# Two decoder layers on one core: weight matrices laid out block by block in DRAM

## The chip, the cores and the metric

The kernel runs on one core of a Trainium2 chip. The metric is the time of one execution on the device in microseconds (us), as a median of several runs. One further execution was profiled. Its trace gives the span from the first to the last instruction, what each engine did and waited for, and what the 16 DMA engines moved.

## The reference, cut to what matters

Two decoder layers, width 2048, sequence 256, all in float32. In each layer the input is scaled and shifted by vectors that come from a conditioning vector `c`, goes through a token mixer with 16 heads, and is added back through a gate and normalized. An MLP with hidden width 8192 does the same.

```python
c_act = jax.nn.silu(c)
for l in range(DEPTH):                                   # DEPTH = 2
    mod = c_act @ w_ada[l] + b_ada[l]                    # w_ada[l]: 2048 x 12288
    sh_a, sc_a, g_a, sh_m, sc_m, g_m = jnp.split(mod[:, None, :], 6, axis=-1)
    h = x * (1.0 + sc_a) + sh_a
    y = _mixer(h, ..., w_in[l], ..., w_o[l], ...)        # w_in[l]: 2048 x 6152, w_o[l]: 2048 x 2048
    x = _layernorm(ALPHA * x + (1.0 + g_a) * y, ln1_g[l], ln1_b[l])
    h = x * (1.0 + sc_m) + sh_m
    y = jnp.square(jax.nn.relu(h @ w_up[l])) @ w_down[l] # 2048 x 8192, 8192 x 2048
    x = _layernorm(ALPHA * x + (1.0 + g_m) * y, ln2_g[l], ln2_b[l])
```

The mixer splits `h @ w_in` into queries, keys and values of two groups of 8 heads and, between them, 8 columns of forget gates (`ff`), runs causal attention in both groups, and multiplies the joined heads by `w_o`.

## The kernel before

All weights are read once, in loads of 512 KB, each into a buffer `raw` of 128 partitions x 1024 float32 (4 KB on each partition). There are 7 such buffers (`RAW_BUFS`), used in turn, and every load is issued by SP, so all of them stand in one queue in the order of the program. SP issues a load once the buffer that it goes to has been read for the last time.

There are three kinds of load:

- **Blocks of a weight matrix** (`w_in`, `w_o`, `w_up`, `w_down`): 256 rows by 512 columns. `rows_of` (L348) cuts them out of the row-major matrix, and `wload` (L138) issues them at L140. Row p of the block and row 128+p go to partition p, so a partition gets two runs of 2 KB. There are 768 of them. For each, ACT rounds the block into `wh` (L134), DVE takes the rest into `wl` (L135), and PE runs three matmuls for each product (`mm3` at L302 to L304, `proj_T` at L328 to L331, `up` at L908 and L910), so that the result has nearly full float32 precision. `wh` and `wl` have three buffers each.
- **Scale and shift loads**, `ada_T` (L150, issued at L156): 128 rows of `w_ada`, from each of which two runs of 512 columns are taken, one of the shift and one of the scale, 2048 columns apart. Again two runs of 2 KB for each partition. 256 of them. DVE multiplies each by one element of `c_act` for each partition and adds it up (L146, L148); after 16 loads PE and DVE reduce the sum over the partitions.
- **Gate loads**, `ada_G` (L179, issued at L189): 128 rows of `w_ada`, 1024 neighbouring columns, so one run of 4 KB for each partition. 128 of them, added up by the same line L148.

The blocks set the order of the program. `block` (L289) is called for each of them, and before it issues its load, it lets other work take a step: attention tasks, pieces put off (`later`), and `side_step`, which issues the `w_ada` loads at a rate that is set for each stage (`RATES`). One small load stands apart: `forget` (L697) reads the 8 forget-gate columns of `w_in` at L700, as runs of 32 bytes, 16 of them for each partition.

At the start, 16 scale and shift loads must have been added up before the first `h` can be made. The first three of them are issued, then two loads of `x`, then the bias of `w_ada` (tile `r`, L120), which PE transposes and DVE copies (L124), and only then the other 13.

Of the kernel before, what the change touches and what calls it, by code (L numbers as in the profile page):

```python
# [18 lines left out]
P = 128  # L19
D = 2048  # L20
S = 256
NT = S // P
KT = D // P
DEPTH = 2
HD = 128
NF = 8
# [3 lines left out]
GRP = 2048  # L30
# [7 lines left out]
CW = 512  # L38
OFF_FQ, OFF_FK, OFF_FV = 0, FW, 2 * FW
OFF_FF = 3 * FW  # L40
OFF_DQ = OFF_FF + NF
OFF_DK = OFF_DQ + FW
OFF_DV = OFF_DK + FW
RAW_BUFS = 7
# [26 lines left out]
    return math.ldexp(float(round(m * 2**bits)), e - bits)  # L71

@with_exitstack
def decoder(ctx: ExitStack, tc: tile.TileContext, x, c, positions, w_ada, b_ada, w_in, b_f,
            lambda_q1, lambda_k1, lambda_q2, lambda_k2, subln_g, w_o, ln1_g, ln1_b, w_up, w_down,
            ln2_g, ln2_b, out):
    nc = tc.nc
# [72 lines left out]
    def ada_T(l, vec, kt0):  # L150

        acc = gp.tile([P, 2, CW], F32, tag="acc", name="acc", bufs=1)
        for kt in range(KT):
            raw = wp.tile([P, 2, CW], F32, tag="raw", name="rawa", bufs=RAW_BUFS)
            rows = w_ada[l, kt * P:(kt + 1) * P, :].rearrange("p (v n) -> p v n", n=D)
            nc.sync.dma_start(raw, rows[:, vec:vec + 2, kt0 * P:kt0 * P + CW])  # L156
            ada_add(acc, raw, kt, kt == 0)
            if kt < KT - 1:
                yield 1

        def finish():
            pss = []
            for i in range(2):
                ps = bank()
                for f in range(4):
                    nc.tensor.transpose(ps[:, f * P:(f + 1) * P], acc[:, i, f * P:(f + 1) * P], ident)
                pss.append(ps)
            yield
            for i, ps in enumerate(pss):
                red = sm.tile([P, 4], F32, tag="red", name="red")  # L170
                nc.vector.reduce_sum(red, ps.rearrange("p (f k) -> p f k", f=4), axis=mybir.AxisListType.X)
                s0 = (vec + i) * KT + kt0
                nc.vector.scalar_tensor_tensor(modT[l, vec + i][:, kt0:kt0 + 4], red, float(i),
                                               badaT[l][:, s0:s0 + 4], ALU.add, ALU.add)

        pending[(l, vec, kt0)] = [0, finish()]
        yield 1

    def ada_G(l, vec):  # L179

        gates[l, vec] = []
        for half in range(2):
            c0 = vec * D + half * 1024
            acc = gp.tile([P, 1024], F32, tag="acc", name="acc", bufs=1)
            nc.gpsimd.memset(acc, 0.0)
            nc.sync.dma_start(acc[0:1, :], b_ada[l:l + 1, c0:c0 + 1024])
            for kt in range(KT):
                raw = wp.tile([P, 1024], F32, tag="raw", name="rawa", bufs=RAW_BUFS)
                nc.sync.dma_start(raw, w_ada[l, kt * P:(kt + 1) * P, c0:c0 + 1024])  # L189
                ada_add(acc, raw, kt, False)  # L190
                if kt < KT - 1:
                    yield 1
            hi, lo = split_w(acc.unsqueeze(1), 1, 1024)
            g = g4([P, 1024], f"gate{l}_{vec}_{half}")
            gates[l, vec].append(g)

            def finish(g=g, hi=hi, lo=lo):
                for q in range(2):
                    qs = slice(q * CW, (q + 1) * CW)
                    ps = bank()  # L200
                    nc.tensor.matmul(ps, lhsT=ones_r, rhs=hi[:, 0, qs], start=True, stop=False)
                    nc.tensor.matmul(ps, lhsT=ones_r, rhs=lo[:, 0, qs], start=False, stop=True)
                    nc.scalar.activation(g[:, qs], ps, AF.Identity, bias=one)
                yield

            pending[(l, vec, "gate", half)] = [0, finish()]
            yield 1
# [98 lines left out]
    def proj(po, lhs, wrows, c0, kt0, kt1, first=True, last=True):  # L306

        for kb in range(kt0, kt1, 2):
            wh, wl = block(wrows(kb, 2, c0, CW), 2, CW)
            need_h(kb + AHEAD)  # L310
            for j in range(2):
                kt = kb + j
                for t in range(NT):
                    mm3(po[t], lhs(kt, 0, t), lhs(kt, 1, t), wh[:, j, :], wl[:, j, :],
                        first and kt == kt0, last and kt == kt1 - 1)

    def proj_T(po, hT, wrows, c0, kt0, kt1, first=True, last=True):


        for kb in range(kt0, kt1, 2):  # L320
            wh, wl = block(wrows(kb, 2, c0, CW), 2, CW)
            need_h(kb + AHEAD)
            for j in range(2):
                kt = kb + j
                for f in range(4):
                    cs = slice(f * P, (f + 1) * P)
                    o = po[f // 2][:, (f % 2) * S:(f % 2 + 1) * S]
                    nc.tensor.matmul(o, lhsT=wh[:, j, cs], rhs=hT[:, kt, 0, :],  # L328
                                     start=first and kt == kt0 and f % 2 == 0, stop=False)
                    nc.tensor.matmul(o, lhsT=wh[:, j, cs], rhs=hT[:, kt, 1, :], start=False, stop=False)  # L330
                    nc.tensor.matmul(o, lhsT=wl[:, j, cs], rhs=hT[:, kt, 0, :], start=False,  # L331
                                     stop=last and kt == kt1 - 1 and f % 2 == 1)

    def proj_tail(po, lhs, wrows, c0, kt0, kt1, done):


        room = big.tile([P, 4, 2, 2, CW], F32R, tag="hT", name="room")
        ws = []
        for i, kb in enumerate(range(kt0, kt1, 2)):
            ws.append(block(wrows(kb, 2, c0, CW), 2, CW, (room[:, i, 0], room[:, i, 1]) if i < 4 else None))  # L340
        for t in range(NT):
            for kt in range(kt0, kt1):
                wh, wl = ws[(kt - kt0) // 2]
# [1 line left out]
                mm3(po[t], lhs(kt, 0, t), lhs(kt, 1, t), wh[:, j, :], wl[:, j, :], False, kt == kt1 - 1)  # L345
            done(t)

    def rows_of(w):  # L348
        def f(kb, a, c0, n):
            return w[kb * P:(kb + a) * P, c0:c0 + n].rearrange("(a p) n -> p a n", p=P)  # L350
        return f


    mask = const.tile([P, 2, P], F32, name="mask")
# [342 lines left out]
    def forget(l, hT):  # L697

        raw = wp.tile([P, KT, NF], F32, tag="raw", name="fraw", bufs=RAW_BUFS)
        nc.sync.dma_start(raw, w_in[l, :, OFF_FF:OFF_FF + NF].rearrange("(a p) n -> p a n", p=P))  # L700
        wf = wp.tile([P, KT, 2 * NF], F32R, tag="wh", name="wf", bufs=W_BUFS)
        nc.scalar.copy(wf[:, :, 0:NF], raw)
        nc.vector.tensor_sub(wf[:, :, NF:2 * NF], raw, wf[:, :, 0:NF].bitcast(F32))
# [51 lines left out]

    def mixer(l, hT, gate_key, stats, passes, done):

        wr = rows_of(w_in[l])

        def lhs(kt, part, t):  # L760
            return hT[:, kt, part, t * P:(t + 1) * P]
# [109 lines left out]
            return (MXf if kt < 8 else MXd)[:, kt % 8, part, t * P:(t + 1) * P]  # L871

        side_rate(RATES[l][2])
        wo = rows_of(w_o[l])

        def finish(ch, po, t):
            add_gated(po, gate_key, ch, stats, True, [t])
# [16 lines left out]

    def mlp(l, hT, gate_key, stats, done, halves, pieces):

        wu = rows_of(w_up[l])

        def up(c0, kt0, kt1):
            pu = [mm(), mm(), bank(), bank()]  # L900
            for kb in range(kt0, kt1, 2):
                wh, wl = block(wu(kb, 2, c0, CW), 2, CW)
                need_h(kb + AHEAD)
                for j in range(2):
                    kt = kb + j
# [33 lines left out]
        for g in range(NG):  # L939
# [24 lines left out]
            def lhs(kt, part, t):  # L964
                return Hs[kt // 8][:, kt % 8, part, t * P:(t + 1) * P]

            wd = rows_of(w_down[l, g * GRP:(g + 1) * GRP, :])
            last = g == NG - 1
            for ch in range(4):
                po = [mm() for _ in range(NT)]  # L970
# [79 lines left out]
    for l in range(DEPTH):  # L1050
# [30 lines left out]
        mlp(l, hT, (l, 5), old, after, halves if early_up else None, affine_later(ln1_g[l:l + 1], ln1_b[l:l + 1]))  # L1081


_INS = ["x", "c", "positions", "w_ada", "b_ada", "w_in", "b_f", "lambda_q1", "lambda_k1", "lambda_q2",
        "lambda_k2", "subln_g", "w_o", "ln1_g", "ln1_b", "w_up", "w_down", "ln2_g", "ln2_b"]


# [16 lines left out]
```

## Time and profile before

| | |
|---|---|
| Median of 3 runs | 2371.37 us (2369.19 to 2372.78) |
| The profiled execution | 2369.32 us, of which the span is 2367.6 us |
| PE busy | 2281.3 us, 96% of the span |
| DVE, ACT busy | 1790.1 us (76%), 1155.3 us (49%) |
| DMA | 619.37 MB, mean 262 GB/s; packets took 77.6% of the time of 16 engines |
| Mean granted TensorE clock | 0.994 |

How to read it: PE is TensorE's matmuls, DVE VectorE, ACT ScalarE, SPq the queue of SyncE that issues the DMAs. `a <- b: t, n, m` in a table of waits means that a waited for b, t us in total, n times, m us at the longest. In the chain of waits, each piece is what the next one had to wait for; a DMA in it has its start of issue and the time until it landed. A DMA share is the part of the time in which the mean of the 16 DMA engines had a packet in work; it can read slightly over 1. A clock of 1.00 is the full 2.4 GHz, 0.50 is 1.2 GHz.

### The profile page before, as it was taken

The numbers are of one execution on the slowest core, as the hardware profiler recorded it, in microseconds if no ns is written. First come the engines' busy times: TensorE is split into PE (matmuls) and PEld (weight loads), VectorE is DVE, ScalarE is ACT, GpSimd is POOL, SyncE is SP. The second block draws the span as 40 slices with busy tenths as digits, with TensorE's granted clock in tenths as the row PEclk, the third lists the DMA queues.
The fourth block names the chain that finished last, engine by engine and source line by source line (L and its number), as shares of the span: only waits on it lengthen the run. The fifth ranks groups of instructions, "written<-read, shape, count | busy, mean of one in ns | idle before, by whom it ended". The sixth has DMA issues, their size and how long they took to land.

```text
span 2367.6 us, 33293 instructions
## 1 busy us (share of the span) xinstructions
PE 2281.3 (96%) x12444; PEld 1959.6 (83%) x12444; DVE 1790.1 (76%) x2339; ACT 1155.3 (49%) x1684; POOL 35.1 (1%) x60
## 2 busy tenths in 40 slices
PE   4999999899999999999999999999999999999998
PEld 3878798699989888888777778987888888888886
DVE  7899888988888778888777975667675666555657
ACT  2543675344546345346444663444554553553542
POOL 0000010000000000000000000000000000000000
PEclk9999999999999999999999999999999999999999
DMA  9999688889898888888759877765777777756653
GB/s 344 326 331 308 193 265 305 312 315 325 303 349 301 302 281 309 312 293 300 273 186 303 292 226 234 233 215 170 221 263 251 229 242 240 230 189 195 187 188 123
DMA packets 309890, 619.37 MB, mean 262 GB/s; under 512 B 24200, under 2 KB 25048, under 8 KB 309728
## 3 DMA queue, kind: packets, MB, share of 16 engines
q1 hardware_dynamic: 309728, 617.25, 77.6%
q8 instruction: 97, 1.59, 0.3%
q14 instruction: 65, 0.53, 0.1%
HBM read 615.07 MB, written 2.10 MB: 261 GB/s over the span
## 4 chain that ended last, share of the span: by engine, by line
PE 76%; DVE 9%; DMA 9%; issue 3%; ACT 2%; POOL 0%; SPq 0%; DVEq 0%; ACTq 0%; POOLq 0%
PE mm L303 13%; PE mm L302 13%; PE mm L304 13%; PE mm L908 7%; PE bank L908 7%; DMA rawa<-in_w_ada_dram 5%; PE mm L331 4%; PE mm L330 4%; PE mm L328 4%; PE mm L910 4%; PE bank L910 4%; DVE wl L135 4%; DVE acc L148 2%; DMA raw<-in_w_in_dram 1%; ACT wh L134 1%
## 5 line engine op out<-in xcount | busy, mean ns | idle before, releaser
L134 ACT CAST wh<-raw 128x1024 fp32r<-128x1024 f32 x752 | 789.5, 1052 | 929.5 <-PE mm L304 491.5
L135 DVE TENSOR_TENSOR wl<-raw,wh 128x1024 fp32r<-128x1024 f32 x752 | 913.7, 1221 | 347.2 <-ACT wh L134 343.9
L148 DVE SCALAR_TENSOR_TENSOR acc<-rawa,cact,acc 128x1024 f32<-128x1024 f32 x368 | 471.0, 1280 | 137.8 <-DMA rawa<-in_w_ada_dram 136.5
L303 PE MATMUL mm<-wl,Hs 128*128 128x512 f32 x992 | 386.5, 390 | 2.0 <-DVE wl L135 1.9
L302 PE MATMUL mm<-wh,Hs 128*128 128x512 f32 x992 | 386.2, 389 | 0.0
L304 PE MATMUL mm<-wh,Hs 128*128 128x512 f32 x992 | 386.0, 389 | 0.0
L331 PE MATMUL mm<-hT,wl 128*128 128x256 f32 x1024 | 289.6, 285 | 6.0 <-DVE wl L135 5.4
L328 PE MATMUL mm<-hT,wh 128*128 128x256 f32 x1024 | 290.9, 285 | 1.9 <-DVE hT L486 1.1
L330 PE MATMUL mm<-hT,wh 128*128 128x256 f32 x1024 | 289.8, 284 | 0.2 <-DVE hT L487 0.2
L908 PE MATMUL mm<-hT,wh 128*128 128x512 f32 x768 | 286.7, 396 | 0.5 <-DVE hT L487 0.5
L908 PE MATMUL bank<-hT,wh 128*128 128x512 f32 x768 | 286.2, 395 | 0.0
L303 PEld LDWEIGHTS mm<-wl,Hs 128*128 128x128 f32 x992 | 186.2, 188 | 41.9 <-DVE wl L135 3.5
L302 PEld LDWEIGHTS mm<-wh,Hs 128*128 128x128 f32 x992 | 186.2, 188 | 38.7
L304 PEld LDWEIGHTS mm<-wh,Hs 128*128 128x128 f32 x992 | 186.2, 188 | 38.6
L910 PE MATMUL mm<-hT,wl 128*128 128x256 f32 x768 | 215.5, 281 | 0.2 <-DVE wl L135 0.2
L910 PE MATMUL bank<-hT,wl 128*128 128x256 f32 x768 | 215.3, 280 | 0.0
L302 PE MATMUL mm<-wh,hT 128*128 128x512 f32 x512 | 200.8, 400 | 5.9 <-DVE hT L486 5.7
L303 PE MATMUL mm<-wl,hT 128*128 128x512 f32 x512 | 203.4, 397 | 3.1 <-DVE wl L135 2.7
L331 PEld LDWEIGHTS mm<-hT,wl 128*128 128x128 f32 x1024 | 196.0, 192 | 8.7 <-DVE wl L135 8.3
L304 PE MATMUL mm<-wh,hT 128*128 128x512 f32 x512 | 200.9, 393 | 0.0
L328 PEld LDWEIGHTS mm<-hT,wh 128*128 128x128 f32 x1024 | 196.8, 192 | 3.4 <-DVE hT L486 1.3
L330 PEld LDWEIGHTS mm<-hT,wh 128*128 128x128 f32 x1024 | 197.1, 192 | 0.8 <-DVE hT L487 0.4
(248 smaller groups left out, 2665.7 us busy)
## 6 DMA issues: line engine op xcount, KB each, us to landing
rawa<-in_w_ada_dram SPq DMA_DIRECT2D x384, 512.0 KB, 5.5
raw<-in_w_up_dram SPq DMA_DIRECT2D x256, 512.0 KB, 4.8
raw<-in_w_down_dram SPq DMA_DIRECT2D x256, 512.0 KB, 5.1
raw<-in_w_in_dram SPq DMA_DIRECT2D x192, 512.0 KB, 5.4
raw<-in_w_o_dram SPq DMA_DIRECT2D x64, 512.0 KB, 4.6
gb<-in_ln_g_dram SPq DMA_DIRECT2D x12, 256.0 KB, 5.5
bb<-in_ln_b_dram SPq DMA_DIRECT2D x12, 256.0 KB, 5.3
xacc<-in_x_dram SPq DMA_DIRECT2D x8, 256.0 KB, 6.7
```

The costliest lines, as they stand in the source:

```text
L134: nc.scalar.copy(wh, raw)
L135: nc.vector.tensor_sub(wl, raw, wh.bitcast(F32))
L148: nc.vector.scalar_tensor_tensor(acc, raw, k, acc, ALU.mult, ALU.add)
L302: nc.tensor.matmul(o, lhsT=hi, rhs=wh, start=start, stop=False)
L303: nc.tensor.matmul(o, lhsT=hi, rhs=wl, start=False, stop=False)
L304: nc.tensor.matmul(o, lhsT=lo, rhs=wh, start=False, stop=stop)
L328: nc.tensor.matmul(o, lhsT=wh[:, j, cs], rhs=hT[:, kt, 0, :], start=first and kt == kt0 and f % 2 == 0, stop=False)
L330: nc.tensor.matmul(o, lhsT=wh[:, j, cs], rhs=hT[:, kt, 1, :], start=False, stop=False)
L331: nc.tensor.matmul(o, lhsT=wl[:, j, cs], rhs=hT[:, kt, 0, :], start=False, stop=last and kt == kt1 - 1 and f % 2 == 1)
L908: nc.tensor.matmul(pu[f], lhsT=wh[:, j, cs], rhs=hT[:, kt].rearrange("p a s -> p (a s)"), start=kt == kt0, stop=False)
L910: nc.tensor.matmul(pu[f][:, 0:S], lhsT=wl[:, j, cs], rhs=hT[:, kt, 0, :], start=False, stop=kt == kt1 - 1)
```

## The change

The host stores the weights in another order, and the kernel reads them in that order. `w_in` (without its 8 forget-gate columns), `w_o`, `w_up` and `w_down` become arrays of blocks: block [column group of 512][pair of 128-row groups] holds [128 partitions][2][512], as it will stand in `raw`. A block is then 512 KB in one piece, and each partition's part is a run of 4 KB. `w_ada` is split into two arrays, one for the scale and shift loads (`w_ada_T`, [partition][2][512] for each load) and one for the gate loads (`w_ada_G`, [partition][1024] for each load), both in one piece of 512 KB for each load. The forget-gate columns become an array `w_f` with 512 bytes in one run for each partition. The loads, their sizes, their tiles, their order and all computation stay as they were.

```diff
-OFF_DQ = OFF_FF + NF
+OFF_DQ = OFF_FF
...
-            rows = w_ada[l, kt * P:(kt + 1) * P, :].rearrange("p (v n) -> p v n", n=D)
-            nc.sync.dma_start(raw, rows[:, vec:vec + 2, kt0 * P:kt0 * P + CW])
+            nc.sync.dma_start(raw, w_ada_T[l, vec // 3, kt0 // 4, kt])
...
-                nc.sync.dma_start(raw, w_ada[l, kt * P:(kt + 1) * P, c0:c0 + 1024])
+                nc.sync.dma_start(raw, w_ada_G[l, vec // 3, half, kt])
...
-            wh, wl = block(wrows(kb, 2, c0, CW), 2, CW)
+            wh, wl = block(wrows(kb, c0), 2, CW)
...
-    def rows_of(w):
-        def f(kb, a, c0, n):
-            return w[kb * P:(kb + a) * P, c0:c0 + n].rearrange("(a p) n -> p a n", p=P)
-        return f
+    def blocks_of(w, first=0):
+
+        return lambda kb, c0: w[c0 // CW, (first + kb) // 2]
...
-        nc.sync.dma_start(raw, w_in[l, :, OFF_FF:OFF_FF + NF].rearrange("(a p) n -> p a n", p=P))
+        nc.sync.dma_start(raw, w_f[l])
...
-            wd = rows_of(w_down[l, g * GRP:(g + 1) * GRP, :])
+            wd = blocks_of(w_down[l], g * GRP // P)
...
+def _blocks(w):
+
+    l, k, n = w.shape
+    return w.reshape(l, k // 256, 2, P, n // CW, CW).transpose(0, 4, 1, 3, 2, 5)
+
+
+def _laid_out(inputs):
+
+    t = dict(inputs)
+    a = t.pop("w_ada")
+    a = a.reshape(DEPTH, KT, P, 2, 3, D)
+    t["w_ada_T"] = a[:, :, :, :, 0:2].reshape(DEPTH, KT, P, 2, 2, 4, CW).transpose(0, 3, 5, 1, 2, 4, 6)
+    t["w_ada_G"] = a[:, :, :, :, 2].reshape(DEPTH, KT, P, 2, 2, D // 2).transpose(0, 3, 4, 1, 2, 5)
+    w = t["w_in"]
+    t["w_f"] = w[:, :, OFF_FF:OFF_FF + NF].reshape(DEPTH, KT, P, NF).transpose(0, 2, 1, 3)
+    t["w_in"] = _blocks(np.concatenate([w[:, :, :OFF_FF], w[:, :, OFF_FF + NF:]], axis=2))
+    for name in ("w_o", "w_up", "w_down"):
+        t[name] = _blocks(t[name])
+    return t
```

The new order is made on the host before the launch, outside the time measured.

## Rows read from the trace of the kernel before

**Rows 1.** The page: span, and DMA packets of the whole execution.

```profile
span 2367.6 us, 33293 instructions
...
DMA packets 309890, 619.37 MB, mean 262 GB/s; under 512 B 24200, under 2 KB 25048, under 8 KB 309728
```

**Rows 2.** Waits of PE over the whole span, two rows.

```profile
PE mm L303 <- DVE wl L135: 6.4, 8, 1.7
...
PE mm L331 <- DVE wl L135: 5.4, 5, 2.0
```

**Rows 3.** Waits of PE in six stretches, one row each, in order of time.

```profile
PE mm L303 <- DVE wl L135: 1.7, 1, 1.7
...
PE mm L303 <- DVE wl L135: 1.5, 1, 1.5
...
PE mm L303 <- DVE wl L135: 1.2, 2, 0.9
...
PE mm L303 <- DVE wl L135: 1.5, 3, 0.8
...
PE mm L331 <- DVE wl L135: 3.6, 3, 2.0
...
PE mm L331 <- DVE wl L135: 1.4, 1, 1.4
```

**Rows 4.** The chain of waits in order of time: start us, us, what.

```profile
3.93 7.23 DMA r<-in_b_ada_dram
...
250.85 5.22 DMA raw<-in_w_in_dram
...
444.09 1.21 DVE xacc L497 x2
...
1131.54 5.96 DMA rawa<-in_w_ada_dram
...
1248.83 5.64 DMA rawa<-in_w_ada_dram
...
1307.49 6.59 DMA raw<-in_w_in_dram
...
1440.54 5.65 DMA raw<-in_w_in_dram
...
1525.44 5.48 DMA rawa<-in_w_ada_dram
```

**Rows 5.** Lines L156 and L189: issue ns min/median/max, and time to landing.

```profile
L156 SPq DMA_DIRECT2D rawa<-in_w_ada_dram x256: 367/368/554, 1.3 to 1555.3; - x128
...
DMA to landing us min/median/max: 3.5/5.6/10.4
...
L189 SPq DMA_DIRECT2D rawa<-in_w_ada_dram x128: 327/341/933, 200.1 to 2009.1; - x128
...
DMA to landing us min/median/max: 3.4/5.4/7.6
```

**Rows 6.** Busy time by stretch; last three columns: granted clock, DMA share, GB/s.

```profile
0.00:237.00 237.00, 200.38 (x1024) 167.56 (x1025) 202.61 (x243) 96.88 (x121) 5.04 (x29) 1.00 0.95 327
...
500.00:560.00 60.00, 59.86 (x501) 59.62 (x500) 49.15 (x47) 25.39 (x31) 0.00 (x0) 1.00 0.97 343
...
660.00:690.00 30.00, 30.00 (x134) 24.84 (x133) 25.36 (x26) 13.36 (x16) 0.00 (x0) 1.00 1.01 374
...
1340.00:1400.00 60.00, 59.10 (x304) 46.98 (x302) 49.20 (x126) 39.02 (x102) 4.65 (x4) 1.00 0.73 223
```

**Rows 7.** The same view, three short stretches (first time: PE busy).

```profile
1448.00:1452.00 4.00, 4.00 (x23) 4.00 (x22) 1.68 (x2) 0.23 (x1) 0.00 (x0) 0.57 0.95 309
260.00:268.00 8.00, 7.07 (x26) 4.88 (x25) 7.99 (x28) 4.15 (x12) 0.00 (x0) 0.79 0.44 136
...
1242.00:1244.00 2.00, 2.00 (x10) 1.67 (x9) 2.00 (x3) 0.78 (x1) 0.00 (x0) 1.00 0.73 84
```

**Rows 8.** DMA queue in 2160 to 2240 us, then in 2265 to 2325 us.

```profile
q1 hardware_dynamic: 7817, 15.09, 64.1%
...
q1 hardware_dynamic: 5925, 11.41, 56.3%
```

More of the change, by code (lines that the diff above doesn't have):

```diff
@@ L73, in decoder @@
 @with_exitstack
-def decoder(ctx: ExitStack, tc: tile.TileContext, x, c, positions, w_ada, b_ada, w_in, b_f,
+def decoder(ctx: ExitStack, tc: tile.TileContext, x, c, positions, w_ada_T, w_ada_G, b_ada, w_in, w_f, b_f,
             lambda_q1, lambda_k1, lambda_q2, lambda_k2, subln_g, w_o, ln1_g, ln1_b, w_up, w_down,
@@ L320, in proj_T @@
         for kb in range(kt0, kt1, 2):
-            wh, wl = block(wrows(kb, 2, c0, CW), 2, CW)
+            wh, wl = block(wrows(kb, c0), 2, CW)
             need_h(kb + AHEAD)
@@ L339, in proj_tail @@
         for i, kb in enumerate(range(kt0, kt1, 2)):
-            ws.append(block(wrows(kb, 2, c0, CW), 2, CW, (room[:, i, 0], room[:, i, 1]) if i < 4 else None))
+            ws.append(block(wrows(kb, c0), 2, CW, (room[:, i, 0], room[:, i, 1]) if i < 4 else None))
         for t in range(NT):
@@ L756, in mixer @@
     def mixer(l, hT, gate_key, stats, passes, done):
-        wr = rows_of(w_in[l])
+        wr = blocks_of(w_in[l])
         def lhs(kt, part, t):
@@ L873, in mixer @@
         side_rate(RATES[l][2])
-        wo = rows_of(w_o[l])
+        wo = blocks_of(w_o[l])
         def finish(ch, po, t):
@@ L895, in mlp @@
     def mlp(l, hT, gate_key, stats, done, halves, pieces):
-        wu = rows_of(w_up[l])
+        wu = blocks_of(w_up[l])
         def up(c0, kt0, kt1):
@@ L901, in up @@
             for kb in range(kt0, kt1, 2):
-                wh, wl = block(wu(kb, 2, c0, CW), 2, CW)
+                wh, wl = block(wu(kb, c0), 2, CW)
                 need_h(kb + AHEAD)
@@ L1081, in decoder @@
         mlp(l, hT, (l, 5), old, after, halves if early_up else None, affine_later(ln1_g[l:l + 1], ln1_b[l:l + 1]))
-_INS = ["x", "c", "positions", "w_ada", "b_ada", "w_in", "b_f", "lambda_q1", "lambda_k1", "lambda_q2",
-        "lambda_k2", "subln_g", "w_o", "ln1_g", "ln1_b", "w_up", "w_down", "ln2_g", "ln2_b"]
+_INS = ["x", "c", "positions", "w_ada_T", "w_ada_G", "b_ada", "w_in", "w_f", "b_f", "lambda_q1", "lambda_k1",
+        "lambda_q2", "lambda_k2", "subln_g", "w_o", "ln1_g", "ln1_b", "w_up", "w_down", "ln2_g", "ln2_b"]
+def _blocks(w):
[13 more added lines that the diff above has]
+    return t
 def kernel(**inputs):
@@ L1093 @@
     arrays, args = {}, []
+    inputs = _laid_out(inputs)
     for name in _INS:
```

## The prediction

> **What bounds the kernel now.** I read the page first: the table of the time before has PE busy for 96% of the span, and 619 MB moved by DMA engines that are busy for 77.6% of it [rows 1]. Both are near their ends, so the question is which of them still makes the other wait. The chain of waits puts some 9% of the span on DMAs, but a chain shows one tight path, and another may stand right behind it. So I went from the chain to PE's own waits. A faster load can shorten the run only where PE stands still, or where its clock falls, because a load is late.
>
> PE's waits for weights are waits for `wl`, the last thing made from a block: 6.4 and 5.4 us, 13 times in all [rows 2]. Six stretches hold 10.9 of these 11.8 us [rows 3]: 440 to 450 us (1.7), 1100 to 1150 (1.5), 1224 to 1275 (1.2), 1300 to 1320 (1.5), 1405 to 1450 (3.6) and 1500 to 1560 (1.4). The reader is to see how small that is: a queue that moves 619 MB costs PE about 12 us in 2368. In the stretch 0 to 237 us the DMA engines are busy for 95% of the time, and still no such wait is among the six [rows 6].
>
> For each stretch I then asked the chain of waits, in order of time, what stands ahead of the late `wl` [rows 4]. Five times it is a run of loads, each issued when the one before it had been used up: 4 loads up to the one at 1131.54, 5 up to 1248.83, one of `w_in` at 1307.49 (behind broadcasts of layer-norm rows that the change doesn't touch), 5 up to 1440.54, 4 up to 1525.44. In the first stretch it is not a load: DVE is adding into `xacc` (444.09), one instruction behind the other. Those 1.7 us are not the change's to win.
>
> **The change part by part.** *Packets.* Before, 309890 − 25048 = 284842 packets have 2 KB or more [rows 1]. If each run is one packet, the 1024 loads with runs of 2 KB make 262144, the 128 gate loads with runs of 4 KB 16384; that leaves 6314, which fits the 40 loads of `x` and layer-norm rows and the 8 stores of the output (128 packets each, 6144), and a few. So a run of 4 KB is one packet already in this kernel. The 1024 loads become 131072 packets. The total should be 309890 − 131072 − 2 x (2048 − 128) for the forget gates = 174978.
>
> *SP's issue.* It takes 368 ns for a load in 2 KB runs and 341 ns for a gate load [rows 5]: 27 ns x 1024 = 28 us less on SP, which mostly waits for free buffers. I count nothing of its own; if that cover is gone, it is 0.03 us for each load in the sums below.
>
> *A load's time to land.* The trace has no load in one piece of 512 KB, so I bound it. Below: gate loads (4 KB runs) land at best in 3.4 us, scale and shift loads (2 x 2 KB) in 3.5; medians 5.4 and 5.6 [rows 5]. That is 0.1 us of gain for each load. Nothing at all would be the same case. Above: with the queue full, 500 to 560 us moves 343 GB/s at a share of 0.97 with 2 KB runs only, 354 GB/s for a full share; 660 to 690, where 7 of 19 weight loads have 4 KB runs, moves 374 at 1.01, 370 for a full share; 1340 to 1400, with `w_in`, whose rows start at odd places, has 223 at 0.73, only 305 [rows 6]. A lone load's 3.5 us holds 524 KB at 354 GB/s = 1.5 us of transfer, so some 2.0 us don't scale, and of a median 5.6 us about 3.5 do (its own transfer and the queue ahead). If `w_in`'s 305 becomes 370, that is 18% of 3.5 = 0.6 us for each load. I take the middle, 0.35 us: the stretches that matter are mostly `w_in` stages in layer 1, but the queue there also holds scale and shift loads, whose two rates are closer.
>
> The Trainium skill bears on this in "DMA: Bandwidth & Descriptors", section "Why small descriptors are slow (HBM only)": a fixed cost of about 3 cycles for each packet of 32-byte beats. By it, as an estimate, 2 x 67 cycles become 131, 2.2% less, under the 0.1 us of the rows, and the sum would be that of the second rival. The same page (section on the iDMA fabric) has a stream of 1 MiB loads in 4 KiB rows at 408.7 GB/s; by it, as an estimate, the sum would be nearer to the first rival's. No run here shows either.
>
> *The runs of loads.* Each loses 0.35 us a load, up to the wait that it ends in. 1100: 4 loads, 1.4 of 1.5. 1224: 5 loads, 1.75, so all 1.2. 1300: one load, 0.35. 1405: 5 loads, 1.75 of 3.6. 1500: 4 loads, 1.4 of 1.4. Together 6.1 us. The 0.9 us outside the six stretches I leave.
>
> *The clock.* After the wait of 2.0 us that ends the stretch 1405 to 1450, the granted clock is 0.57 in 1448 to 1452 [rows 7]: near the lower level (1.2 GHz) for most of 4 us, (1 − 0.57) x 4 = 1.7 us lost. If the wait shrinks, the clock may hold. I take half, 0.85 us.
>
> *Attention of layer 0.* A load of `w_in` at 250.85 is on the chain [rows 4]; in 260 to 268 us PE then idles 0.93 us and has a clock of 0.79, another 1.7 us [rows 7]. One load: 0.35 us; at most all 2.6.
>
> *Start.* `r` is issued at 3.93 and lands 7.23 us later, behind three scale and shift loads [rows 4]; DVE can't go on adding before it has `r`'s transpose. Three loads at 0.1 to 0.2 us of transfer: I take 0.3 us, at most 0.6.
>
> *Forget gates.* 2048 packets of 32 bytes become 128 of 512. In 1242 to 1244 us the engines show a share of 0.73 for 84 GB/s [rows 7]; at 354 GB/s those bytes need 0.24, so about 1 us of queue is freed, twice. The first time nothing waits for it; the second time it helps the stretch at 1224, which is counted in full. Nothing here; with the lower bound for a load it adds 0.7.
>
> *Elsewhere.* DVE, ACT and PE do the same instructions in the same order, and no wait is added. Where PE waits for layer norms or for DVE, an earlier load changes nothing.
>
> The sum: 6.1 + 0.85 + 0.35 + 0.3 = 7.6 us. The profiled execution took 2369.3 us, 1.7 more than its span and 2.1 less than the median of the runs. Against it that is 2361.7; the forecast for the median is 2371.4 − 7.6 = 2363.8 us. With 0.1 us for each load: 0.4 + (0.5 + 0.7) + 0.1 + 0.5 + 0.4 + 0.1 + 0.1 = 2.8 us. With everything that a load can be blamed for: 1.5 + 1.2 + 1.5 + 3.6 + 1.4 + 0.9 + 1.7 + 2.6 + 0.6 = 15.0 us.
>
> **The rivals.** *First, all late loads vanish:* 15.0 us, 2356.4. For it: the waits are short and stand at the ends of long runs, so a small gain for each load ends them; only the 3.6 us need more. Against it: the broadcasts and the fixed 2 us stay.
>
> *Second, the loads are hidden anyway:* 2.8 us, 2368.6, which is no change by this kernel's measurement (0.2%, 4.7 us). For it: 3.4 against 3.5 us is the only pair of like loads in the trace, and the busiest stage of all, 0 to 237 us, has no wait for a block among the six [rows 3, 6].
>
> *Third, slower, by addresses:* what a packet of 2 KB costs depends on where it lies. `w_up` alone (rows 32 KB apart) has 7817 packets in 80 us at 64.1%, 105 ns each; `w_down` (8 KB apart) 5925 in 60 us at 56.3%, 91 ns [rows 8]. If all 16 engines reading out of one piece of 512 KB are worse off by those 15%, the stretch 0 to 237 us needs 0.95 x 1.15 = 1.09 of its time, 22 us more: 2393. It decides from about 5% on, where the share of 0.95 reaches 1. Against it: in the pair, the closer rows are the cheaper ones.
>
> That the change does not do what it says I rule out: the kernel already has 4 KB packets where source and tile are in one run.
>
> **How the numbers follow.** Forecast 0.48, own range 2360 to 2367; first rival 0.14; second 0.29; third 0.09. All of the first and most of the forecast (0.44) are faster by over 4.7 us: 0.58. The second and the rest of the forecast are the same: 0.33. Slower: 0.09. The range goes from the first rival, less 2 us for the spread of the runs, 2354, to the second with the runs' spread and a little of no gain at all, 2372; above it lies mainly the third.
>
> **What would show it.** Packets near 175000. The median landing of scale and shift loads falls from 5.6 to about 5.2 us. DMA busy share falls while GB/s at a full share rises to 370 or more. PE's waits for `wl` fall from 11.8 to about 5 us, the one at 440 to 450 stays, and the half clock near 1448 is short or gone. I would be wrong if landing times stay within 0.1 us, if PE's waits move to another place in the same stage as DVE's order takes over, or if the full-share rate falls under 340 GB/s in the first 237 us. I would be wrong the other way if PE's matmuls themselves start closer together, which nothing in the trace says.

## The result

The changed kernel takes 2355.33 us (median of 4 runs, 2353.2 to 2357.31), the kernel before, run beside it, 2372.07 us. The ratio is 0.9927, with a 95% interval of 0.9906 to 0.9947: 0.73% faster, 16.7 us, where 7.6 were forecast. The time lies in the range given, near its lower end and 1.1 us from the first rival's 2356.4.

The profiled execution took 2353.96 us, 1.8 more than its span. Four lines of its page, which answer to [rows 1]; the second gives each engine's busy time, its share of the span and its instructions:

```profile
span 2352.2 us, 33293 instructions
...
PE 2278.0 (97%) x12444; PEld 1958.9 (83%) x12444; DVE 1791.8 (76%) x2339; ACT 1156.4 (49%) x1684; POOL 35.1 (1%) x60
...
DMA packets 174978, 619.36 MB, mean 263 GB/s; under 512 B 20105, under 2 KB 21209, under 8 KB 174817
...
q1 hardware_dynamic: 174816, 617.25, 75.5%
```

The packets are exactly the 174978 forecast. PE is busy for 3.3 us less than before and stands still for 74.2 us in place of 86.3 (span less busy time): 12.1 + 3.3 = the 15.4 us by which the span is shorter. Most of the gain is thus PE's idle time, and the next question is which waits it is made of. PE's waits over the whole span, after (`a <- b: us, times, longest`), beside [rows 2]; all lines of the code have moved by one to three:

```profile
PE bank L123 <- DMA r<-in_b_ada_dram: 8.0, 1, 8.0
...
PE mm L303 <- DVE wl L136: 3.1, 4, 1.0
...
PE mm L331 <- DVE wl L136: 2.4, 3, 1.7
...
PE bank L737 <- DVE lf L733: 0.5, 1, 0.5
```

The waits for `wl` fell from 11.8 to 5.5 us, those for the forget gates' `lf` from 2.2 to 0.5, and PE's waits for attention tiles (`s`, `pT`, `o`, labelled DVE or ACT) from 5.9 to 3.8. The wait for `r` fell by 0.4; those for layer norms (`xacc`) stayed at 15.0. The remaining 1.6 us of idle time are spread over rows too small to tell.

The six stretches of [rows 3], after. Those of 1224 to 1275 and 1500 to 1560 us have no wait for `wl` any more; the other four, in order of time:

```profile
PE mm L303 <- DVE wl L136: 1.0, 1, 1.0
...
PE mm L303 <- DVE wl L136: 1.0, 1, 1.0
...
PE mm L303 <- DVE wl L136: 0.7, 1, 0.7
...
PE mm L331 <- DVE wl L136: 2.2, 2, 1.7
```

Loads, answering to [rows 5]: issue ns and the time to landing.

```profile
L156 SPq DMA_DIRECT2D rawa<-in_w_ada_T_dram x256: 327/328/1495, 1.2 to 1541.0; - x128
...
DMA to landing us min/median/max: 3.1/5.2/9.6
...
L189 SPq DMA_DIRECT2D rawa<-in_w_ada_G_dram x128: 327/328/423, 199.6 to 1994.0; - x128
...
DMA to landing us min/median/max: 3.1/5.0/7.4
```

The scale and shift loads land 0.4 us earlier, as forecast. But so do the gate loads (5.4 to 5.0), whose runs were 4 KB already, 48 KB apart. Not all of that is their own order: with only the blocks and forget gates changed (an experiment below), they land at 5.0 us too. A load also gains from what stands ahead of it in the queue. By the page's list of issues the medians of the blocks went from 5.4 to 4.8 us (`w_in`), 5.1 to 4.5 (`w_down`), 4.8 to 4.7 (`w_up`) and 4.6 to 4.6 (`w_o`).

Busy time by stretch, answering to [rows 6, 7]; the last three columns are granted clock, DMA share and GB/s:

```profile
0.00:237.00 237.00, 200.91 (x1026) 167.95 (x1027) 202.72 (x243) 97.07 (x121) 5.04 (x29) 1.00 0.92 329
500.00:560.00 60.00, 59.87 (x501) 59.64 (x500) 49.38 (x51) 27.41 (x34) 0.00 (x0) 1.00 0.93 355
660.00:690.00 30.00, 30.00 (x134) 24.83 (x133) 26.00 (x26) 13.82 (x16) 0.00 (x0) 1.00 0.99 368
1340.00:1400.00 60.00, 59.83 (x293) 47.49 (x294) 47.48 (x120) 37.93 (x97) 3.73 (x4) 0.97 0.65 218
1448.00:1452.00 4.00, 4.00 (x36) 4.00 (x35) 3.35 (x3) 2.14 (x3) 0.00 (x0) 1.00 0.88 305
```

For a full share that is 329 / 0.92 = 358 GB/s in the first 237 us (before 344), 382 in 500 to 560 (354), 372 in 660 to 690 (370) and 335 in 1340 to 1400 (305). The half clock near 1448 us is gone, but 1340 to 1400 now reads 0.97 where it was 1.00.

**Where the time came from.** All four engines run the same instructions in the same order in both kernels, so the same PE instruction can be looked up in both timelines. The table gives by how much it starts earlier, and what each stretch (times of before) adds.

| stretch, us | lead at its end, us | added | forecast |
|---|---|---|---|
| 0 to 255, start | 0.5 | 0.5 | 0.3 |
| 255 to 284, attention of layer 0 | 2.4 | 1.9 | 0.35 |
| 284 to 472 | 4.4 | 2.0 | 0 |
| 472 to 1101 | 4.5 | 0.1 | 0 |
| 1101 to 1222 | 4.8 | 0.3 | 1.4 |
| 1222 to 1260 | 6.6 | 1.8 | 1.2 |
| 1260 to 1325 | 9.75 | 3.1 | 0.35 |
| 1325 to 1428 | 7.9 | -1.8 | 0 |
| 1428 to 1497, with the wait of 1405 to 1450 | 11.1 | 3.2 | 1.75 + 0.85 |
| 1497 to 1551 | 12.85 | 1.7 | 1.4 |
| 1551 to the end | 15.4 | 2.6 | 0 |

Some of these steps are the clock's. Before, 1.7 us each were lost in 260 to 268 and in 1448 to 1452 [rows 7]; after, both stretches read 1.00. In turn the clock after reads 0.72 in 1340 to 1344 and 0.86 in 1344 to 1348, (0.28 + 0.14) x 4 = 1.7 us lost, where before has 1.00. PE had stood still for 0.9 us just before that (a wait for the attention tile `s`); before has the same 0.9 us in 1348 to 1352 and no such fall behind it. I have no explanation for that.

### The profile page after: what moved, and what is told of

The parts are those of the page before. It is cut to its first block, busy times and chain, and to the rows that moved or that the text cites. A ratio compares the mean times of both kernels' runs of the same rounds, so it can differ in the third digit from the quotient of the medians.

```text
span 2352.2 us, 33293 instructions
## 1 busy us (share of the span) xinstructions
PE 2278.0 (97%) x12444; PEld 1958.9 (83%) x12444; DVE 1791.8 (76%) x2339; ACT 1156.4 (49%) x1684; POOL 35.1 (1%) x60
## 2 busy tenths in 40 slices
DMA packets 174978, 619.36 MB, mean 263 GB/s; under 512 B 20105, under 2 KB 21209, under 8 KB 174817
## 4 chain that ended last, share of the span: by engine, by line
PE 85%; DVE 7%; DMA 4%; issue 2%; ACT 2%; POOL 0%; SPq 0%; DVEq 0%; ACTq 0%; POOLq 0%
PE mm L303 15%; PE mm L302 15%; PE mm L304 15%; PE mm L907 7%; PE bank L907 7%; PE mm L331 5%; PE mm L330 5%; PE mm L328 5%; PE mm L909 4%; PE bank L909 4%; DVE wl L136 2%; DVE acc L149 2%; DMA raw<-in_w_in_dram 1%; DMA rawa<-in_w_ada_G_dram 1%; DMA rawa<-in_w_ada_T_dram 1%
## 5 line engine op out<-in xcount | busy, mean ns | idle before, releaser
L136 DVE TENSOR_TENSOR wl<-raw,wh 128x1024 fp32r<-128x1024 f32 x752 | 914.8, 1222 | 350.4 <-ACT wh L135 348.1
L149 DVE SCALAR_TENSOR_TENSOR acc<-rawa,cact,acc 128x1024 f32<-128x1024 f32 x368 | 471.2, 1280 | 118.8 <-DMA rawa<-in_w_ada_T_dram 66.8
```

The costliest lines, as they stand in the source:

```text
L136: nc.vector.tensor_sub(wl, raw, wh.bitcast(F32))
L149: nc.vector.scalar_tensor_tensor(acc, raw, k, acc, ALU.mult, ALU.add)
```

## The experiments

The theory with which I went in: loads land earlier, and each late one that anything on PE's path waits for gives back its share. Its rivals: it is the length of the runs (fewer, longer packets); it is where the addresses lie (one piece of 512 KB); it is only one kind of load; it is DVE's order, in which an addition that waits for a `w_ada` load holds up what stands behind it. The letters of the theories are those of the texts put on record before each run.

| kernel | ratio to the kernel before | 95% interval | PE idle in its profile, us |
|---|---|---|---|
| the change | 0.9927 | 0.9906 to 0.9947 | 74.2 |
| one piece, runs of 2 KB | 0.9939 | 0.9924 to 0.9954 | 73.1 |
| far apart, runs of 4 KB | 0.9973 | 0.9962 to 0.9985 | 83.0 |
| only `w_ada` changed | 0.9973 | 0.9961 to 0.9986 | 81.6 |
| only blocks and forget gates | 0.9968 | 0.9957 to 0.9979 | 80.4 |
| only forget gates | 0.9998 | 0.9984 to 1.0013 | 86.2 |
| before, 8 buffers | 0.9988 | 0.9977 to 0.9999 | 80.7 |
| the change, 8 buffers | 0.9930 | 0.9918 to 0.9942 | 71.7 |
| the change, additions later | 0.9932 | 0.9912 to 0.9951 | 75.4 |
| the change, bias later | 0.9918 | 0.9903 to 0.9933 | 74.4 |

The last column, span less busy time, follows the ratios but for the kernel before with 8 buffers, while PE's busy time wanders from 2274.2 to 2289.5 us without order, since falls of the clock, at 1.7 us or a multiple for each, come at other places in each profile.

**One piece, but two runs of 2 KB.** Each load is one piece of 512 KB; a partition's two runs lie 256 KB apart in it. The array of the scale and shift loads (`w_ada_T`) is laid out to match; that line is not shown.

```diff
-            nc.sync.dma_start(raw, w_ada_T[l, vec // 3, kt0 // 4, kt])
+            nc.sync.dma_start(raw, w_ada_T[l, vec // 3, kt0 // 4, kt].rearrange("a p n -> p a n"))
...
-    return w.reshape(l, k // 256, 2, P, n // CW, CW).transpose(0, 4, 1, 3, 2, 5)
+    return w.reshape(l, k // 256, 2, P, n // CW, CW).transpose(0, 4, 1, 2, 3, 5)
```

> Every load of blocks and of scale and shift is one piece of 512 KB, but within it the two 128-row halves stand one behind the other, so a partition still has two runs of 2 KB. Theory A (the gain is that of fewer, longer packets): packets go back up to about 306050, landing of scale and shift loads stays near 5.6 us, ratio to the kernel before 0.998 to 1.001. Theory B (the gain is where the bytes lie: one piece in place of rows far apart): landing about 5.2 us, ratio 0.992 to 0.995.

Measured: 0.9939, 2357.03 us. The packets are 306050, nearly those of before, and SP's issue takes 368 ns again. PE's waits for `wl`:

```profile
PE mm L303 <- DVE wl L136: 2.7, 3, 1.0
...
PE mm L331 <- DVE wl L136: 0.3, 1, 0.3
```

Scale and shift loads land at a median of 5.3 us, blocks (L141) at 4.5. So 0.61 of the 0.73% come without a single longer run, and the change's interval holds this ratio: that runs of 4 KB add to one piece is not shown.

**Runs of 4 KB, but far apart.** Each partition's run is 4 KB, and the runs of one load lie 16 to 64 KB apart, with the other column groups of the same rows between them. Below are the lines for the blocks; the two `w_ada` arrays are changed in the same way.

```diff
-        return lambda kb, c0: w[c0 // CW, (first + kb) // 2]
+        return lambda kb, c0: w[(first + kb) // 2, :, c0 // CW]
...
-    return w.reshape(l, k // 256, 2, P, n // CW, CW).transpose(0, 4, 1, 3, 2, 5)
+    return w.reshape(l, k // 256, 2, P, n // CW, CW).transpose(0, 1, 3, 4, 2, 5)
```

> Runs of 4 KB for each partition, but the runs of one load are 16 to 64 KB apart, not in one piece. Theory A (longer packets): 174978 packets, landing about 5.2 us, ratio 0.992 to 0.995, like the change. Theory B (one piece): landing near 5.6 us, ratio 0.998 to 1.001.

Measured: 0.9973, 2366.42 us, with the change's 174978 packets and its 328 ns for an issue. The waits for `wl` are no shorter than before (12.4 us with a third row of 1.1, `up`; before, 12.0 with 0.2 there):

```profile
PE mm L303 <- DVE wl L136: 7.3, 7, 1.7
...
PE mm L331 <- DVE wl L136: 4.0, 4, 1.9
```

The intervals of these two kernels don't touch. Runs of 4 KB at these distances give 0.27%, one piece with short runs 0.61%; each gives something, and one piece gives more.

**Which loads.** Only `w_ada` in the new order, and only the blocks and forget gates:

```diff
-        return lambda kb, c0: w[c0 // CW, (first + kb) // 2]
+        return lambda kb, c0: w[(first + kb) * P:(first + kb + 2) * P, c0:c0 + CW].rearrange("(a p) n -> p a n", p=P)
```

> Only w_ada in the new order; the blocks and the forget gates as before. Theory Q (all loads share one queue, so every load that gets cheaper helps whoever waits): 256 of the 1024 loads change their runs, so about a quarter of the gain, ratio 0.997 to 0.999. Theory D (DVE stands before w_ada loads, and what is behind it in DVE's order is late): most of the gain, ratio 0.993 to 0.995, DVE's waits for rawa down from 136.5 us to about 118.

```diff
-            nc.sync.dma_start(raw, w_ada_T[l, vec // 3, kt0 // 4, kt])
+            rows = w_ada[l, kt * P:(kt + 1) * P, :].rearrange("p (v n) -> p v n", n=D)
+            nc.sync.dma_start(raw, rows[:, vec:vec + 2, kt0 * P:kt0 * P + CW])
...
-                nc.sync.dma_start(raw, w_ada_G[l, vec // 3, half, kt])
+                nc.sync.dma_start(raw, w_ada[l, kt * P:(kt + 1) * P, c0:c0 + 1024])
```

> Only the weight blocks and the forget gates in the new order, w_ada as before. Theory Q: three quarters of the gain, ratio 0.994 to 0.996. Theory D: little, ratio 0.998 to 1.000, DVE's waits for rawa stay near 136 us.

Measured: 0.9973 and 0.9968, gains of 0.27 and 0.32%. Their sum, 0.59%, lies within the change's interval: the two halves add up within what can be measured, and neither kind of load is the cause by itself. Theory Q had the first right and missed the second (0.994 to 0.996): 384 loads of `w_ada` give nearly as much as 768 blocks. Theory D missed both. The second kernel says something about DVE. Its wait for `w_ada` loads, below the same row of the kernel before, is as long as ever, and still it gains:

```profile
DVE acc L148 <- DMA rawa<-in_w_ada_dram: 136.5, 101, 4.5
```

```profile
DVE acc L149 <- DMA rawa<-in_w_ada_dram: 136.0, 105, 3.9
```

So a shorter wait of DVE for these loads is not needed for a gain, as far as one profile tells.

**Only the forget gates' array.**

```diff
-        nc.sync.dma_start(raw, w_in[l, :, OFF_FF:OFF_FF + NF].rearrange("(a p) n -> p a n", p=P))
+        nc.sync.dma_start(raw, w_f[l])
```

> Kernel before, only the 8 forget-gate columns from an array of their own (128 runs of 512 bytes in place of 2048 of 32 bytes). It frees about 1 us of the queue, twice. Theory: only the second stands ahead of waits of PE (1.2 us), ratio 0.9993 to 1.0000. Rival (its packets are a large part of the gain): ratio 0.997 or less.

Measured: 0.9998. These 2048 packets of 32 bytes for each layer are hidden, as forecast.

**More buffers, before and after.** An eighth buffer for loads lets SP issue each earlier without changing how it lands. Room for it comes from two other pools.

```diff
-RAW_BUFS = 7
+RAW_BUFS = 8
...
-E1_BUFS = 8
-E2_BUFS = 5
+E1_BUFS = 7
+E2_BUFS = 4
```

> Kernel before with 8 load buffers in place of 7 (and one fewer small buffer each of two kinds, 7 for 8 and 4 for 5, to make room). A load can be issued one buffer earlier, about 1.2 to 1.4 us, with the order in DRAM as it was. Theory L (what costs is loads that land late by a microsecond or less): ratio 0.991 to 0.995, waits of PE for wl under 5 us, like the change. Theory R (what costs is the rate of the queue, which an eighth buffer does not raise): ratio 0.998 to 1.001.

> Changed kernel with 8 load buffers, as above. Theory L: nearly all lateness is gone already, what is left is PE's 5.5 us for wl and a few us in attention; ratio to the kernel before 0.989 to 0.992. Theory R: as the change, 0.992 to 0.994. If the smaller small buffers cost, above 0.994.

Measured: 0.9988 for the old order and 0.9930 for the new. Theory R held both times. An eighth buffer gives 0.12% (its interval allows up to 0.23) where the new order gives 0.73, and on top of the new order it shows no gain. What the new order gives is thus not had by issuing earlier. Two things limit this test: no run has the smaller pools alone, so a cost of theirs may hide a part, and single waits say little. With 8 buffers in the new order PE's waits for `wl` fell from 5.5 to 1.7 us, and the kernel got no faster.

**DVE's additions later.** In the changed kernel the addition of a `w_ada` load (`ada_add`) is put behind the split of the next block, so that a late `w_ada` load holds up one `wl` less.

```diff
-            ada_add(acc, raw, kt, kt == 0)
+            add_soon(acc, raw, kt, kt == 0)
...
-        return wload(src, a, b, into)
+        r = wload(src, a, b, into)
+        add_now()
+        return r
```

> Changed kernel, but DVE's addition of a w_ada load is written behind the split of the weight block whose turn it is, not ahead of it. Theory D (what is left of PE's waits comes from DVE standing before w_ada loads): ratio to the kernel before 0.989 to 0.992, waits of PE for wl under 3 us. Rival (the additions now hold the load buffers longer, so the queue runs dry): ratio 0.994 or more.

Measured: 0.9932, no better than the change, and between the two forecasts. The waits for `wl` are 5.0 us (under 3 was expected), but one for `s` grew from 1.5 to 3.8. What remains of the waits is not mended by this one exchange.

**The bias later.** At the start, `r` is issued behind the tenth scale and shift load instead of the third.

```diff
-            bias_T(0)
+            while side:
+                if len(badaT) == 0 and adds[0] == 7:
+                    bias_T(0)
+                adds[0] += 1
+                side_pop()
```

> Changed kernel, but the bias of w_ada (tile r) is loaded behind the tenth of the first 16 scale and shift loads, not behind the third, so that DVE does not stand still for it between its first and second addition. Theory S (the start is a chain of r and 15 additions of 1.3 us): 4 to 5.5 us less, ratio to the kernel before 0.990 to 0.9915. Rival (additions wait for their loads instead, which land no faster than DVE adds them): under 2 us less, ratio 0.992 to 0.993.

Measured: 0.9918, between the two forecasts; the change's interval holds it. In the profile the first reduction of the scale and shift sums (L171) starts at 29.9 us in place of 32.4, so 2.5 us are won at the start; DVE then waits three times, 3.5 us in all, for the loads themselves (row below, first 40 us). PE's idle time over the whole span is that of the change (74.4 against 74.2 us), since its waits for `wl` are 7.4 us here in place of 5.5. A gain is plausible, but 0.1% is less than these intervals can tell.

```profile
DVE acc L149 <- DMA rawa<-in_w_ada_T_dram: 3.5, 3, 2.0
```

**Loads alone, queue full.** Seven buffers, one order of loads after another.

> No layers are computed: x goes to the output, and then loads of 512 KB follow one another on the one queue, 8 alone (each waits for the one before) and 64 in a row into 7 buffers for each of eight orders in DRAM: w_up, w_down, w_in, scale and shift loads and gate loads as before; w_up in one piece with runs of 2 KB; runs of 4 KB 64 KB apart; one piece with runs of 4 KB. Theory A (packets): the two orders with 4 KB runs and the gate loads are equal and 3 to 12% faster per load than the others, the piece with 2 KB runs is not. Theory B (addresses): both pieces are fastest and within 3% of each other, w_up as before (rows 32 KB apart) and the 4 KB runs 64 KB apart are slowest. Lone loads differ by 0.1 to 0.4 us in the same order.

The six parts with a full queue, in order: `w_in` in rows, scale and shift loads, gate loads, one piece with runs of 2 KB, runs of 4 KB far apart, one piece with runs of 4 KB. The last three columns are clock, DMA share and GB/s:

```profile
350.00:425.00 75.00, 0.00 (x0) 1.00 1.05 387
435.00:510.00 75.00, 0.00 (x0) 1.00 1.05 387
525.00:590.00 65.00, 0.00 (x0) 1.00 1.03 410
605.00:680.00 75.00, 0.00 (x0) 1.00 1.05 387
690.00:760.00 70.00, 0.00 (x0) 1.00 1.03 409
775.00:845.00 70.00, 0.00 (x0) 1.00 1.03 410
```

Theory A held. With a full queue only the length of a run counts in these six: 387 GB/s for 2 KB and 410 for 4 KB, wherever they lie. That is 6%. (The rows of `w_up` and `w_down` have no such part; their loads were mixed with the ones meant to be alone.) The Trainium skill's fixed cost for each packet ("DMA: Bandwidth & Descriptors", section "Why small descriptors are slow (HBM only)") would have made it 2.2%, as an estimate; the measurement decides. The 410 agrees with the same page's 408.7 GB/s for a stream of 1 MiB loads in 4 KiB rows (section on the iDMA fabric). The part of this kernel that was meant for lone loads can't be read: other loads were in flight beside them.

**Loads alone, one at a time.** One buffer, so that each load waits for the one before it.

> No layers are computed: x goes to the output, then 24 loads of 512 KB for each of the eight orders in DRAM follow one another through one single buffer, so that each starts when the one before has landed: the queue never holds more than one. Theory F (two effects: how far apart the rows lie sets the time of a load when few are in flight, the length of the runs sets the rate when the queue is full): both orders in one piece land in 3.0 to 3.2 us, with 2 KB and with 4 KB runs alike; w_up, w_ada and the 4 KB runs 64 KB apart in 3.4 to 3.8. Rival (runs alone): all three orders with 4 KB runs equal and 0.1 us or more under all with 2 KB runs.

Measured, medians to landing of 24 loads each: `w_up` 3.6 us, `w_down` 3.5, `w_in` 3.7, scale and shift 3.6, gates 3.5, one piece with runs of 2 KB 3.6, far apart with runs of 4 KB 3.4, one piece with runs of 4 KB 3.2. Theory F had one piece with runs of 2 KB land earlier even when it is alone; that fell. So did its rival, by which the three orders with runs of 4 KB are equal: they land at 3.2, 3.4 and 3.5. A hole was left: alone and with a full queue, one piece with short runs gains nothing, and in the kernel it gains most.

**Loads alone, four, three and two in flight.** So the last run looked between the two. How many loads are in flight in the kernel's own stages, on average, can be estimated from the rows as GB/s x landing / 524288 bytes: before, 327 x 5.8 us gives 3.6 in the first 237 us, which has no late block, and in the stages that wait, 272 x 5.15 gives 2.7 (1225 to 1400 us) and 241 x 4.8 gives 2.2 (1400 to 1570).

> Leaves out both layers: it only loads, and copies x to the output, so that its time says nothing of the kernel. Seven orders of loads, 24 loads each, with 4, then 3, then 2 loads in flight: w_down in rows 8 KB apart, one piece with runs of 2 KB, runs of 4 KB that lie 16 KB apart, one piece with runs of 4 KB, w_up in rows 32 KB apart, w_in in rows 24 KB apart, scale and shift loads. Theory A (with a few loads in flight it matters where a load's addresses lie): with 2 in flight both orders in one piece land within 0.2 us of each other, and w_down's rows and the far runs of 4 KB at least 0.4 us later, as in the stage 2080 to 2130 us of the kernels (4.2 against 3.2 to 3.3 us). Theory B (only the length of a run matters, whatever is in flight): the two orders with runs of 4 KB land within 0.2 us of each other at every depth and before all with runs of 2 KB, by 0.1 us at 2 in flight and by 6% at 4; the stage's 4.2 against 3.3 us then comes from something that loads alone don't have. Both expect about 2.6 to 3.2 us for each load in transfer and overlap at 2 in flight, that is landings of 3.2 to 4.5 us, and a full queue's 387 or 410 GB/s at 4 in flight if transfers alone set the rate.

Lines of the view by source line, two in flight: `w_down` in rows (L67), one piece with runs of 2 KB (L69), far apart with runs of 4 KB (L71), one piece with runs of 4 KB (L73):

```profile
L67 SPq DMA_DIRECT2D raw<-in_w_down_dram x24: 367/368/368, 526.5 to 577.4; - x24
...
DMA to landing us min/median/max: 3.5/4.6/5.2
L69 SPq DMA_DIRECT2D raw<-in_dn_2k_dram x24: 367/368/368, 579.4 to 627.7; - x24
...
DMA to landing us min/median/max: 4.0/4.1/4.5
L71 SPq DMA_DIRECT2D raw<-in_dn_far_dram x24: 327/328/341, 629.6 to 683.4; - x24
...
DMA to landing us min/median/max: 4.3/4.7/5.1
L73 SPq DMA_DIRECT2D raw<-in_dn_4k_dram x24: 327/328/328, 686.1 to 734.2; - x24
...
DMA to landing us min/median/max: 3.3/4.3/4.5
```

All medians to landing, in us; the column for one is from the run before, where the far order and the two in one piece were made of `w_up`, here of `w_down`:

| order | 1 in flight | 2 | 3 | 4 |
|---|---|---|---|---|
| `w_down` in rows, 2 KB | 3.5 | 4.6 | 5.6 | 5.4 |
| far apart, 4 KB | 3.4 | 4.7 | 5.5 | 5.1 |
| one piece, 2 KB | 3.6 | 4.1 | 4.8 | 5.4 |
| one piece, 4 KB | 3.2 | 4.3 | 5.0 | 5.1 |
| `w_in` in rows, 2 KB | 3.7 | 4.5 | 5.4 | 5.4 |
| scale and shift, 2 KB | 3.6 | 4.5 | 5.5 | 5.4 |
| `w_up` in rows, 2 KB | 3.6 | 4.2 | 4.8 | 5.4 |

With four in flight the length of a run decides (5.1 against 5.4). With two or three the place decides: `w_down`'s rows and the far runs of 4 KB land together, both orders in one piece land 0.3 to 0.8 us before them, and the longer run gives nothing. Theory A held but for one pair: with two in flight both pieces land within 0.2 us of each other, and rows and far runs 0.5 and 0.4 us behind the piece with runs of the same length (only `w_down`'s rows against the piece with 4 KB stay under its 0.4, at 0.3). `w_up` lands like one piece although its rows are 32 KB apart, so "in one piece" is not the rule itself, and what is stays open.

The table agrees with the change's medians by kind: rows of `w_up` land no later than one piece with 4 KB at two and three in flight (4.2 and 4.8 against 4.3 and 5.0), and in this pair of kernels `w_up` gained 0.1 us; `w_down` lands 0.3 and 0.6 us later there, and gained 0.6; scale and shift loads 0.2 and 0.5, and gained 0.4. `w_in` (0.2 and 0.4) gained more, 0.6.

The Trainium skill has a loss for rows at large powers of two ("DMA: Bandwidth & Descriptors", section "Latency and other measured facts"), measured at 512 KiB to 8 MiB apart, which it puts down, as an inference, to rows that fall on the same memory channels. No run here tests that. Among the distances tried here, `w_up` at 32 KB beside `w_down` at 8 KB doesn't look like a simple rule by distance.

**How this shows in the kernels.** Medians of the 49 to 52 `w_in` loads in 1225 to 1400 us: 5.2 us before, 5.0 and 5.3 in the two other kernels that read them and `w_ada` in rows (only forget gates; 8 buffers), 4.7 far apart with 4 KB, 5.0 in one piece with 2 KB, 4.8 with only `w_ada` changed, 5.0 with only the blocks, 4.5 in the change, and 4.6, 4.7 and 4.7 in its three variants. Here the far runs land before the short runs in one piece, against the order of the two ratios, so in this stage the medians don't bear out that the place decides. One caution: a single profile can mislead by as much. In 2080 to 2130 us `w_down` lands at 4.3 us before and at 3.2 after, which looks like 1.1 us of gain; but the three kernels that read it in the old rows with one thing changed elsewhere have 3.5 there (far apart it takes 4.2). In one piece it takes 3.1 to 3.2 in all six kernels, so 0.3 us is the order's, and the other 0.8 belong to that profile of before, for no cause that I found.

## Why the prediction was right in sign and half the size

*Packets, issue, forget gates:* 174978 packets and nothing for the forget gates (0.9998), as forecast. An issue went from 368 to 328 ns, a little below the 341 forecast.

*A load's time to land:* taken at 0.35 us. The medians fell by 0.4 (scale, shift and gates) and 0.6 (`w_in`, `w_down`), inside the bounds of 0.1 and 0.6; those of `w_up` and `w_o` fell by 0.1 and 0.0, which I had not told apart. The reason behind the number was wrong in part: I derived it from the rate of a full queue, as a matter of transfer alone. In the stages that wait, two to three loads are in flight, and there the place of the rows costs, 0.3 to 0.8 us for `w_down` by the loads alone.

*The runs of loads:* 6.1 us, and the waits for `wl` fell by 6.3, to 5.5 us (about 5 was forecast). That the totals agree is partly luck, since the parts miss on both sides: 1100 to 1150 gave 0.5 in place of 1.4, 1405 to 1450 gave 1.4 in place of 1.75, 1300 to 1320 gave 0.8 in place of 0.35, and 440 to 450, which was to stay, fell from 1.7 to 1.0.

*The clock:* half of 1.7 us was counted near 1448, and all of it came. Another 1.7 us came at 260 to 268, which I had only as part of an upper bound, and 1.7 were lost anew at 1340. Net 1.7 in place of 0.85. Since such falls move about from profile to profile, this term is a draw from a spread of some us more than a consequence.

*The step that failed* is in "Elsewhere": "Where PE waits for layer norms or for DVE, an earlier load changes nothing." The waits labelled DVE or ACT (`lf` and the attention tiles) fell by 1.7 + 2.1 = 3.8 us, and the stretches 284 to 472 and 1551 to the end, which have nothing in the forecast, gave 2.0 + 2.6. A label names the engine that came last, not what it had waited for. For `wl` I had followed DVE's order back to a load; for these waits I had not. (The half on layer norms held: 15.0 us before and after.) PE's wait in 1224 to 1275 us:

```profile
PE bank L738 <- DVE lf L734: 1.7, 1, 1.7
```

The chain of waits of the kernel before (start us, us, what) shows how a load stands behind it:

```profile
1265.68 5.32 DMA rawa<-in_w_ada_dram
...
1271.02 1.28 DVE acc L148
1272.31 0.09 DVE u L726
...
1274.06 0.17 DVE lf L734
...
1274.63 0.38 PE bank L738
```

DVE adds a `w_ada` load as soon as it has landed and waits again at the next one. Whatever stands behind such an addition in DVE's order comes late, here the steps that make `lf`, and PE waits for it under DVE's name. How late DVE is adds up over several loads. DVE's waits for `w_ada` loads ahead of this `lf`, before in 1252 to 1272 us and, for the same additions, after in 1246 to 1264.5:

```profile
DVE acc L148 <- DMA rawa<-in_w_ada_dram: 6.3, 5, 2.6
```

```profile
DVE acc L149 <- DMA rawa<-in_w_ada_T_dram: 4.5, 4, 2.2
```

DVE stands still 1.8 us less, and PE's wait of 1.7 us is gone. In the two other stretches, waits for the attention tiles `s` (0.6 us at 397) and `pT` (1.0 us at 1568) are gone; 0.7 and 0.4 us there are shorter waits for `wl`. Over the whole span DVE's waits for `w_ada` loads (L148) were 136.5 us before and are 66.8 + 50.7 = 117.5 after.

That much is read from two traces. By experiment it is not shown: moving the additions in the changed kernel gained nothing, and the blocks alone gain with DVE's wait at 136.0. Single waits of this kind vary, too. `lf` is 2.0 us in one piece with 2 KB and 3.3 in the change with 8 buffers, at ratios of 0.9939 and 0.9930. Over all profiles, by the rows of the tables of waits, `lf` and the attention tiles together cost 8.1, 7.9 and 7.3 us in the three kernels that read blocks and `w_ada` in rows, and 4.3 to 6.5 in the five that read everything in one piece. So a fall under these names repeats, at some 2 us on average, and the 3.8 of this pair are more than its usual size. The waits for `wl` are 9.1 to 13.1 us in those three and 1.7 to 7.4 in the five. What is shown most plainly is the sum: PE's idle time is 86 us with rows (80.7 with 8 buffers), 80 to 83 with half of the change or far runs, and 72 to 75 in all five kernels that read everything in one piece.

*The rivals.* The first, that all late loads vanish, gave nearly the time measured, but not by its mechanism: 5.5 of its 11.8 us of `wl` waits are still there, and the clock and waits under DVE's name made up for them. The second (hidden) is excluded by the interval. The third had addresses matter, and they do, with the other sign: no run shows a loss from all engines reading out of one piece, and in the first 237 us the DMA share fell from 0.95 to 0.92.

*What stays open:* which property of the addresses counts with two or three loads in flight; why `w_down` landed at 4.3 us in the one profile of before; and 4.6 us between the 12.1 us of idle time and the 16.7 of the runs. Busy time gives 3.3 of them in this pair, of which 1.7 are the clock, and it wanders by more than that between profiles.

The lowest ratio is that of the change with the bias later, 0.9918 (2355.47 us), but its interval and the change's hold each other's middle.

## What to carry to other kernels

A stage that waits for loads is rarely one with a full queue: work out how many loads are in flight from GB/s x landing time, and take the price of a load from that depth, since the full queue's rate and the lone load's time can both miss it. Lay out a weight so that each load is one piece of DRAM; here that gave more than longer runs did. Before a wait under another engine's name is called safe from a change to the loads, follow that engine's own order back: a load may stand in front.

## What the runs showed of the hardware that I had not expected

- For `w_down` in runs of 2 KB, the place of the rows mattered only at two and three loads of 512 KB in flight (4.6 and 5.6 us in rows against 4.1 and 4.8 in one piece); with one (3.5 and 3.6, the piece made of `w_up`) or four (5.4 and 5.4) it did not. `w_up`'s rows land within 0.1 us of the piece with runs of 2 KB at every depth.
- Three loads of `w_down` in rows in flight land later than four do (5.6 against 5.4 us), and move less: 301 against 383 GB/s.
- SP's issue takes 328 to 341 ns (medians by line) for a load with one run of 4 KB for each partition and 368 to 378 for two of 2 KB, whether they lie in one piece or apart.
